# Scores of all eight attention heads from split, stacked float32r operands in a hybrid encoder block

## The chip, the core and the metric

The kernel runs on one core of a Trainium2 chip. The metric is the device time of one execution in microseconds (us). Several executions are made and the median is given; one more is recorded by the profiler, and all rows below come from that one.

## What is computed

One layer of a streaming encoder on x of 512 tokens by 1024 channels, in float32:

```python
x = x + 0.5 * swiglu_ffn(rms_norm(x, ffn1_norm), ffn1_w13, ffn1_w2)
h = rms_norm(x, mix_norm)
a, g, q, k, v, fl = split(h @ w_in)
y_conv = conv_module(a, g, ...)        # GLU, causal depthwise conv of width 31, LayerNorm, swish
y_attn = forgetting_attention(q, k, v, fl + forget_b)
y = concat(rms_norm(y_conv), rms_norm(y_attn))
x = x + y @ w_out
x = x + 0.5 * swiglu_ffn(rms_norm(x, ffn2_norm), ffn2_w13, ffn2_w2)
out = rms_norm(x, final_norm)
```

The attention has 8 heads of 64 channels. For each block of 128 queries, the scores against all keys up to the end of the block are q k^T / 8 plus the difference of a running sum of log sigmoid gates; a causal mask, a softmax and the product with the values follow. The feed-forward width is 2816.

## The kernel before, in words

Activations lie with channels on the 128 partitions and the 512 tokens in the free dimension. Every large product is made of float32r matmuls: each operand is split into a high part `h`, the value rounded to float32r, and a remainder `l`, and the product is `hi*h + hi*l + lo*h`, three matmuls for each 128 channels. Weights arrive by DMA in tiles `raw`; ScalarE writes `whi`, VectorE subtracts to get `wlo`.

The order of the work is made by a planner (`Plan`). Each operation is recorded with an estimated price; `schedule` walks through time, and gives each engine the operation that can start soonest, and among equals the one with the longest path behind it, raised by an urgency. The result is a fixed order of instructions for each engine, so an instruction whose input is late holds up everything behind it on its engine. Tiles have tags with a number of buffers, handed out in the order in which the program names them.

The stage in the middle goes, in `ORDER`, "c0 c1 c2 c3 v a0 a1 n a2 a3 w0 w1 w2 w3": four tiles of the convolution, the values and gates, attention for pairs of heads 0 and 1, the norm of the convolution, attention for pairs 2 and 3, and the output projection. Convolutions 0 and 2 are made of taps that ScalarE scales (`tap`) and GpSimd adds (`acc`); convolutions 1 and 3 (`DVE_CONV`) are taps that VectorE adds up in PSUM (`conv`), copied by ScalarE into `acc` at the end. The gates go through some twenty small steps on VectorE (`e`, `lf`, `lfs`), are transposed on TensorE (`pc`), summed (`cum`), written to memory and read back spread over the partitions (`ck`). `conv_norm` begins with the sums `ssq_mean` on TensorE over the four finished convolutions, and ends with the split tiles `yh`, `yl` in slots 0 to 7, which the first half of the output projection (`wo`) reads.

`attention(i)` handles a pair of heads, head 0 of the pair on partitions 0 to 63 and head 1 on 64 to 127. Products `pq` and `pk` make q and k for both. For pairs that are not in `STACK` each head gets a float32 q tile of 128 partitions whose other half is zero, so that one float32 matmul with the k tile `kn` of both heads gives the scores of one head. For pairs in `STACK`, the 128 partitions of a head's q tile hold the high part of q on the head's own half and the remainder on the other; k becomes two tiles, `h` with the high part of k on both halves and `l` with the remainder of k on the own half and zeros on the other. Two float32r matmuls, with `h` and with `l`, give qh kh + ql kh + qh kl. They run over at least 256 columns. The mask is added by a third, bfloat16, matmul into the same bank. A softmax follows: one VectorE operation that adds `ck` and takes the minimum (`sm<-s,ck`), an exponential on ScalarE, a scaling, transposes (`pt`) on TensorE, copies (`pT`), and the product with the values (`po`).

"r" slots: the tiles of `slot(n)` have one buffer each. Slots 0 to 21 hold the hidden activations of each half of a feed-forward; in the middle stage 0 to 15 hold `yh` and `yl`, 16 to 19 the convolutions and later k of pair 3, 14, 20 and 21 parts of the gates. Pair 2 keeps its k in the tags u0 to u3, which held the inputs of the convolution.

All operations are recorded through one helper, line 217, so the rows below are told apart by the names of their tiles, not by lines.

Of the kernel before, what the change touches and what calls it, by code (L numbers as in the profile page):

```python
# [25 lines left out]
F32R = mybir.dt.float32r  # L26
# [5 lines left out]
P = 128  # L32
T = 512
# [19 lines left out]
PIECE = 2  # L53
WARM = 10
DVE_CONV = (1, 3)
STACK = (2, 3)
STORES = {1: 0, 4: 2, 7: 5}


# [17 lines left out]
def f32(ap):  # L77
    return ap.bitcast(F32)
# [262 lines left out]
def block_kernel(ctx: ExitStack, tc, x_d, w13a, w2a, wag, wvf, wqk, wo, w13b, w2b, par_d, out_d):  # L341
# [9 lines left out]
    def tile_(shape, tag, name, bufs=1, dt=F32):  # L351
        return plan.tile(sb, shape, dt, tag, name, bufs)

    def bank(tag, name, bufs=1):
        return plan.tile(pp, [P, T], F32, tag, name, bufs)

    def product_bank(name):
        return bank("mm", name, 3)

    def slot(n, name, dt=F32):  # L360

        return tile_([P, T], f"r{n}", name, 1, dt)
# [37 lines left out]
    for w13, w2 in ((w13a, w2a), (w13b, w2b)):  # L400
# [3 lines left out]
        if w13 is w13a:  # L404
            for piece in ORDER.split():
                n = int(piece[1:] or 0)
# [6 lines left out]
    def unit():  # L413
        i = taken[0]
        taken[0] += 1
        src, idx, k, c = units[i]
        raw = tile_([P, k, c], "raw", f"raw{i}", LOADS)
        hi = tile_([P, k, c], "whi", f"whi{i}", SPLITS, F32R)
        lo = tile_([P, k, c], "wlo", f"wlo{i}", SPLITS, F32R)
        load_and_split(i, raw, hi, lo, 0, k)  # L420
        return hi, lo
# [10 lines left out]
    def split(hi, lo, src, gain):  # L432
        S.activation(hi, src, AF.Copy, scale=gain)
        V.scalar_tensor_tensor(lo, src, gain, f32(hi), ALU.mult, ALU.subtract)
# [77 lines left out]
    def product(ps, w, ah, al):  # L512

        hi, lo = w
        n = len(ah)
        first = None
        for k in range(n):
            step = plan.join("PE", first)
            if first is None:
                first = step  # L520
                if taken[0] > 3 or ready == []:
                    in_turn(step)
            PE.matmul(ps, hi[:, k], ah[k], start=k == 0, stop=False)
            PE.matmul(ps, hi[:, k], al[k], start=False, stop=False)
            PE.matmul(ps, lo[:, k], ah[k], start=False, stop=k == n - 1)
            plan.join(None)
        stream[:] = [step]
# [223 lines left out]
    def attention(i):  # L751
        rstd = mix["rstd"]
        plan.urgency = URGENT_Q
        ps = product_bank(f"pq{i}")
        product(ps, unit(), xh, xl)

        halves = [(slice(b * HD, (b + 1) * HD), slice((1 - b) * HD, (2 - b) * HD)) for b in range(2)]
        stacked = i in STACK  # L760
        qs, ks = [], []
        if stacked:
            qn = tile_([P, T], "ew", f"qn{i}", BUFS["ew"])
            V.scalar_tensor_tensor(qn, ps, -(HD ** -0.5), rstd, ALU.mult, ALU.mult)
        for b, (own, other) in enumerate(halves):
            w = tile_([P, T], f"q{i % 2}{b}", f"q{i}{b}", 1, F32R if stacked else F32)
            qs.append(w)
            if stacked:
                S.copy(w[own], qn[own])
                V.tensor_sub(w[other], qn[own], f32(w[own]))  # L770
            else:
                G.memset(w[other], 0.0)
                V.scalar_tensor_tensor(w[own], ps[own], -(HD ** -0.5), rstd[own], ALU.mult, ALU.mult)
        ps = product_bank(f"pk{i}")
        product(ps, unit(), xh, xl)
        kn = tile_([P, T], "k", f"k{i}", 2)
        V.tensor_mul(kn, ps, rstd)
        for b, (own, other) in enumerate(halves):
            if stacked:
                h, l = (tile_([P, T], f"u{2 * b + n}", f"k{i}{b}{n}", 1, F32R) if i % 2 == 0 else  # L780
                        slot(16 + 2 * b + n, f"k{i}{b}{n}", F32R) for n in range(2))
                G.memset(f32(l)[other], 0.0)
                S.copy(h[own], kn[own])
                V.tensor_sub(l[own], kn[own], f32(h[own]))
                G.tensor_copy(h[other], h[own])
                ks.append((h, l))
            else:
                ks.append((kn,))

        plan.urgency = URGENT  # L790
        ck = []
        for b in range(2):
            h = 2 * i + b
            ck.append(tile_([P, T], "ck", f"ck{h}", 2))
            with plan.urgent(500.0):
                Q.dma_start(out=ck[b], in_=cum[h // 4][h % 4:h % 4 + 1, :].spread(P))
        po = bank("misc", f"po{i}", MISC) if i == 0 else bank("cv", f"po{i}")
        for q in range(NT):
            L = (q + 1) * P
            tq = slice(q * P, L)  # L800
            pT = []
            for b in range(2):
                h = 2 * i + b
                ps = bank("s", f"s{h}_{q}", 2)
                plan.join("PE")
                n = max(L, 2 * P) if stacked else L
                for k in ks[b]:
                    PE.matmul(ps[:, :n], qs[b][:, tq], k[:, :n], start=k is ks[b][0], stop=False)
                PE.matmul(ps[:, tq], ident16, mask16, start=False, stop=True)
                plan.join(None)  # L810
                s = tile_([P, T], "sm", f"sm{h}_{q}", BUFS["sm"])[:, :L]
                st3 = tile_([P, 3], "st3", f"st{h}_{q}", 6)
                mn, sm, rs = (st3[:, n:n + 1] for n in range(3))
                V.tensor_tensor_reduce(s, ps[:, :L], ck[b][:, :L], 1.0, 3.0e38, ALU.add, ALU.min, mn)
                S.activation(s, s, AF.Exp, bias=mn, scale=-1.0, accum_out=sm)
                V.reciprocal(rs, sm)
                V.tensor_scalar(s, s, rs, None, ALU.mult)
                pt = bank("pt", f"pt{h}_{q}", PT)
                plan.join("PE")
                for kb in range(q + 1):  # L820
                    PE.transpose(pt[:, kb * P:(kb + 1) * P], s[:, kb * P:(kb + 1) * P], ident)
                plan.join(None)
                pT.append(tile_([P, T], "pT", f"pT{h}_{q}", BUFS["pT"])[:, :L])
                S.copy(pT[b], pt[:, :L])

            plan.join("PE")
            for kb in range(q + 1):
                for b in range(2):
                    h = 2 * i + b
                    PE.matmul(po[b * HD:(b + 1) * HD, tq], vt[:, kb, h * HD:(h + 1) * HD],  # L830
                              pT[b][:, kb * P:(kb + 1) * P], start=kb == 0, stop=kb == q)
            plan.join(None)
        yh[4 + i] = slot(2 * (4 + i), f"yh{4 + i}", F32R)
        yl[4 + i] = slot(2 * (4 + i) + 1, f"yl{4 + i}", F32R)
        split(yh[4 + i], yl[4 + i], po, par[:, G_OA + i:G_OA + i + 1])
        if i < 3:
            attn_stats.add(po)
        else:
            attn_stats.sum(attn_stats.square(po), False)
        plan.urgency = 0.0  # L840
# [39 lines left out]
    for piece in ORDER.split():  # L880
        n = int(piece[1:] or 0)
        if piece[0] == "c":
            conv_tile(n)
        elif piece[0] == "v":
            values()
        elif piece[0] == "a":
            attention(n)
        elif piece[0] == "n":
            plan.urgency = URGENT_LN
            rconv = conv_norm()  # L890
            plan.urgency = 0.0
        else:
            part = n // 2
            if n == 2:
                rattn = attn_stats.rstd()
            for j in range(2):
                w = unit()
                for d in (4 * (n % 2) + 2 * j, 4 * (n % 2) + 2 * j + 1):
                    w_out(part, d, w, rattn if part else rconv)
# [57 lines left out]
```

## Time and profile before

| what | value |
|---|---|
| three runs, us | 983.25, 977.52, 980.85 |
| median, us | 980.85 |
| the profiled execution, us | 982.02 |
| its span, first to last instruction, us | 979.0 |
| mean granted TensorE clock | 0.985 |
| TensorE matmul busy | 953.4 us, 97% of the span |
| VectorE busy | 518.5 us, 53% |
| ScalarE busy | 368.3 us, 38% |
| GpSimd busy | 109.8 us, 11% |
| DMA moved | 91.07 MB, mean 93 GB/s |

The share of an engine over the whole span is a mean over stages: the two feed-forwards (about 0 to 370 and 603 to 979 us) are matmul streams; the middle stage in between is where VectorE, ScalarE and GpSimd are busiest. Matmuls are pipelined and their ends are modelled, so the time between the starts of two matmuls says more than the length shown. PE is TensorE, PEld its weight loads, DVE VectorE, ACT ScalarE, POOL GpSimd. An idle time in brackets stands ahead of an instruction with what ended it. Most scores appear twice, as two records in one row ("x2"): a float32 matmul leaves two, and so do the two float32r matmuls of a stacked score.

### The profile page before, as it was taken

Reading aid. Unit: us, or ns where it says so; the run is one execution under the profiler, and the core shown is the slowest. Engines: PE = TensorE matmul, PEld = TensorE weight load, DVE = VectorE, ACT = ScalarE, POOL = GpSimd, SP = SyncE. Lnnn points to the kernel's source line nnn. Section 1 sums busy time; section 2 is a strip of 40 time slices with the busy share of each in tenths; the row PEclk is TensorE's granted clock in tenths of the full one; section 3 lists DMA queues with packets and bytes.
Section 4 is the critical chain, followed back from the end, with each engine's and each line's share of the span. In section 5 each row is a group of like instructions: output and inputs, shape, how many; then the busy total and the mean of one; then the engine's idle time right before and its main releaser. Section 6 shows DMA issues by size and latency. Waiting matters only on the chain.

```text
span 979.0 us, 11641 instructions
## 1 busy us (share of the span) xinstructions
PE 953.4 (97%) x4687; PEld 777.2 (79%) x4687; DVE 518.5 (53%) x730; ACT 368.3 (38%) x528; POOL 109.8 (11%) x102
## 2 busy tenths in 40 slices
PE   8999999999999999996999999999999999999996
PEld 7888888888888888894666777888888888888885
DVE  6544442244444444989887867444443244444433
ACT  6423221123233325666558655332321122323230
POOL 2000000000000002899432100000000000000000
PEclk9999999999999999999898999999999999999998
DMA  7222332222233222221221212222332222223202
GB/s 242 85 90 104 105 116 88 79 93 101 88 114 118 89 86 74 88 93 71 71 71 34 87 51 80 95 99 89 113 118 90 85 86 89 105 93 132 90 30 87
DMA packets 26838, 91.07 MB, mean 93 GB/s; under 512 B 2840, under 2 KB 6040, under 8 KB 26784
## 3 DMA queue, kind: packets, MB, share of 16 engines
q1 hardware_dynamic: 26784, 90.33, 27.1%
q8 instruction: 36, 0.59, 0.2%
q14 instruction: 18, 0.15, 0.0%
HBM read 88.21 MB, written 2.11 MB: 92 GB/s over the span
## 4 chain that ended last, share of the span: by engine, by line
PE 86%; DVE 6%; ACT 2%; POOL 2%; DMA 1%; issue 1%; SPq 0%; DVEq 0%; POOLq 0%; ACTq 0%
PE f2o L217 12%; PE f2g L217 12%; PE f2u L217 12%; PE f1o L217 12%; PE f1u L217 12%; PE f1g L217 12%; PE wo L217 5%; DVE conv L217 2%; POOL acc L217 2%; PE pg L217 1%; PE pa L217 1%; PE po L217 1%; DVE e L217 1%; DMA x<-x_d 1%; PE s L217 1%
## 5 line engine op out<-in xcount | busy, mean ns | idle before, releaser
L217 ACT CAST whi<-raw 128x1024 fp32r<-128x1024 f32 (+3 forms) x153 | 165.9, 1085 | 476.8 <-issue 223.7
L217 DVE TENSOR_TENSOR wlo<-raw,whi 128x1024 fp32r<-128x1024 f32 (+3 forms) x153 | 198.2, 1296 | 30.8 <-ACT whi L217 29.1
L217 POOL TENSOR_TENSOR acc<-acc,tap 128x512 f32<-128x512 f32 x60 | 88.9, 1482 | 35.0 <-ACT tap L217 30.1
L217 PE MATMUL f2o<-f2ah,whi 128*128 128x512 f32 (+1 forms) x198 | 72.7, 367 | 0.0
L217 PE MATMUL f2o<-f2al,whi 128*128 128x512 f32 (+1 forms) x198 | 72.3, 365 | 0.0
L217 PE MATMUL f2o<-f2ah,wlo 128*128 128x512 f32 (+1 forms) x198 | 72.3, 365 | 0.0
L217 PE MATMUL f1u<-xh,whi 128*128 128x512 f32 x176 | 68.8, 391 | 0.6 <-ACT xh L217 0.6
L217 PE MATMUL f1u<-xl,whi 128*128 128x512 f32 x176 | 68.7, 390 | 0.3 <-DVE xl L217 0.3
L217 PE MATMUL f2g<-xh,whi 128*128 128x512 f32 x176 | 68.7, 390 | 0.0
L217 PE MATMUL f2u<-xh,whi 128*128 128x512 f32 x176 | 68.6, 390 | 0.0
L217 PE MATMUL f1u<-xh,wlo 128*128 128x512 f32 x176 | 68.5, 389 | 0.0
L217 PE MATMUL f2g<-xh,wlo 128*128 128x512 f32 x176 | 68.5, 389 | 0.0
L217 PE MATMUL f2u<-xh,wlo 128*128 128x512 f32 x176 | 68.5, 389 | 0.0
L217 PE MATMUL f2g<-xl,whi 128*128 128x512 f32 x176 | 68.5, 389 | 0.0
L217 PE MATMUL f1o<-f1ah,whi 128*128 128x512 f32 x176 | 68.5, 389 | 0.0
L217 PE MATMUL f1o<-f1al,whi 128*128 128x512 f32 x176 | 68.5, 389 | 0.0
L217 PE MATMUL f1o<-f1ah,wlo 128*128 128x512 f32 x176 | 68.5, 389 | 0.0
L217 PE MATMUL f2u<-xl,whi 128*128 128x512 f32 x176 | 68.5, 389 | 0.0
L217 PE MATMUL f1g<-xh,whi 128*128 128x512 f32 x168 | 65.5, 390 | 0.3 <-ACT whi L217 0.3
L217 PE MATMUL f1g<-xl,whi 128*128 128x512 f32 x168 | 65.5, 390 | 0.0
L217 PE MATMUL f1g<-xh,wlo 128*128 128x512 f32 x168 | 65.5, 390 | 0.0
L217 DVE TENSOR_TENSOR f2un<-f2u,rstd_f2in 128x512 f32<-128x512 f32 x22 | 15.2, 692 | 71.8 <-PE f2u L217 71.8
(231 smaller groups left out, 1768.1 us busy)
## 6 DMA issues: line engine op xcount, KB each, us to landing
raw<-w13b SPq DMA_DIRECT2D x44, 512.0 KB, 3.2
raw<-w13a SPq DMA_DIRECT2D x42, 512.0 KB, 3.3
raw<-w2a SPq DMA_DIRECT2D x16, 704.0 KB, 4.1
raw<-w2b SPq DMA_DIRECT2D x16, 704.0 KB, 4.0
raw<-wag SPq DMA_DIRECT2D x8, 512.0 KB, 3.2
raw<-wqk SPq DMA_DIRECT2D x8, 512.0 KB, 3.2
raw<-wo SPq DMA_DIRECT2D x8, 512.0 KB, 3.2
raw<-wvf SPq DMA_DIRECT2D x4, 520.0 KB, 3.1
```

The source lines that it names most:

```text
L217: ins = getattr(target, method)(*real, **kw)
```

## The change

Pairs 0 and 1 are added to `STACK`, so that their scores are made as those of pairs 2 and 3: q and k are split, the parts are laid one above the other, and two float32r matmuls replace the float32 matmul. The tiles `h` and `l` of k for these two pairs are put into slots 0 to 3 (pair 0) and 4 to 7 (pair 1). Pair 2 keeps its k in u0 to u3 and pair 3 in slots 16 to 19.

```diff
-STACK = (2, 3)
+STACK = (0, 1, 2, 3)
...
             if stacked:
-                h, l = (tile_([P, T], f"u{2 * b + n}", f"k{i}{b}{n}", 1, F32R) if i % 2 == 0 else
+
+                h, l = (slot(4 * i + 2 * b + n, f"k{i}{b}{n}", F32R) if i < 2 else
+                        tile_([P, T], f"u{2 * b + n}", f"k{i}{b}{n}", 1, F32R) if i == 2 else
                         slot(16 + 2 * b + n, f"k{i}{b}{n}", F32R) for n in range(2))
                 G.memset(f32(l)[other], 0.0)
                 S.copy(h[own], kn[own])
```

## Rows read from the trace of the kernel before

**Rows 1.** Busy time per 20 us window; columns name engine, busy us, instructions, clock, DMA.
```profile
440.00:460.00 20.00, 16.56 (x73) 12.49 (x71) 19.89 (x32) 14.75 (x21) 18.00 (x14) 1.00 0.20 71
460.00:480.00 20.00, 14.04 (x55) 11.32 (x56) 17.26 (x29) 5.31 (x12) 8.88 (x7) 0.74 0.33 107
480.00:500.00 20.00, 17.90 (x93) 11.65 (x93) 19.16 (x49) 13.78 (x34) 12.06 (x9) 0.91 0.16 53
500.00:520.00 20.00, 20.00 (x182) 13.84 (x182) 14.55 (x33) 12.55 (x29) 6.22 (x7) 1.00 0.16 53
520.00:540.00 20.00, 17.98 (x107) 11.62 (x107) 16.10 (x39) 18.77 (x34) 5.64 (x6) 0.83 0.09 31
```

**Rows 2.** Chain that ended last, in order of time: start us, us, what.
```profile
495.21 1.13 PE s L217 x3
...
519.57 1.05 PE po L217 x16
```

**Rows 3.** Timeline of TensorE, scores and their masks: start us, us, instruction.
```profile
488.93 0.39 PE L217 MATMUL s<-k,q 128*128 128x128 f32 x2
489.15 0.22 PE L217 MATMUL s<-mask,ident 128*128 128x128 bf16 x1
...
495.21 1.02 PE L217 MATMUL s<-k,q 128*128 128x256 f32 x2 [1.99 <-DVE st L217]
496.03 0.31 PE L217 MATMUL s<-mask,ident 128*128 128x128 bf16 x1
...
506.87 1.02 PE L217 MATMUL s<-k,q 128*128 128x512 f32 x2
507.73 0.22 PE L217 MATMUL s<-mask,ident 128*128 128x128 bf16 x1
...
523.74 0.40 PE L217 MATMUL s<-k,q 128*128 128x256 f32 x2
523.98 0.23 PE L217 MATMUL s<-mask,ident 128*128 128x128 bf16 x1
...
561.48 0.61 PE L217 MATMUL s<-k,q 128*128 128x512 f32 x2
561.94 0.23 PE L217 MATMUL s<-mask,ident 128*128 128x128 bf16 x1
```

**Rows 4.** Groups by form, 380 to 660 us: operation, count, busy us, mean ns.
```profile
L217 DVE SCALAR_TENSOR_TENSOR conv<-u,par,conv 128x512 f32<-128x512 f32 x60 | 44.8, 747 | 0.7
...
L217 DVE TENSOR_TENSOR k<-k,k 64x512 fp32r<-64x512 f32 x4 | 3.4, 860 | 0.1
L217 POOL CAST k<-k 64x512 fp32r<-64x512 f32 x4 | 3.4, 857 | 12.9 <-ACT k L217 12.8
...
L217 DVE TENSOR_TENSOR q<-qn,q 64x512 fp32r<-64x512 f32 x4 | 2.7, 687 | 0.1
L217 DVE SCALAR_TENSOR_TENSOR q<-pq,rstd_f1n 64x512 f32<-64x512 f32 x4 | 2.7, 684 | 0.1
...
L217 ACT CAST k<-k 64x512 fp32r<-64x512 f32 x4 | 2.5, 620 | 0.0
...
L217 POOL MEMSET k<- 64x512 f32 x4 | 2.1, 520 | 7.4 <-DVE conv L217 7.2
...
L217 DVE SCALAR_TENSOR_TENSOR qn<-pq,rstd_f1n 128x512 f32<-128x512 f32 x2 | 1.4, 683 | 2.6 <-PE pq L217 2.6
```

**Rows 5.** Instructions on tile u: count, shortest, median and longest in ns.
```profile
L217 DVE TENSOR_TENSOR u<-an,gn x4: 693/1394/1792, 382.4 to 419.6; 128x512 f32<-128x512 f32 x4
```

**Rows 6.** Timelines of VectorE, ScalarE and TensorE: end of convolution 3, start of the mean.
```profile
501.05 0.75 DVE L217 SCALAR_TENSOR_TENSOR conv<-u,par,conv 128x512 f32<-128x512 f32 x1
...
503.14 0.58 ACT L217 COPY acc<-conv 128x512 f32<-128x512 f32 x1
...
507.88 1.08 PE L217 MATMUL ssq_mean<-acc,mean 128*32 128x128 f32 x32
```

**Rows 7.** Timeline of TensorE: the transposes of the gates.
```profile
466.46 1.12 PE L217 MATMUL pc<-ident,lfs 128*128 128x128 f32 x4 [5.46 <-DVE lfs L217]
```

## The prediction

> **What bounds the kernel now.** The page's busy times first, in the table above: TensorE is busy for 97% of the span, and most of that is the two feed-forwards, which this change does not touch. The middle stage holds the edit. There I read the table of busy time in 20 us windows [rows 1]. From 440 to 500 the engine that never rests is VectorE (19.89, 17.26 and 19.16 of 20 us), while TensorE has holes (16.56, 14.04, 17.90) and part of its time at a lower granted clock (mean 0.74 in 460 to 480, 0.91 in 480 to 500). From 500 to 520 it turns round: TensorE is busy all 20 us and VectorE 14.55. From 520 to 540 TensorE has holes again. So a saving on TensorE before about 495 is a saving on an engine that waits; one after it can be real. The chain of waits says the same: from 495.21, a score of pair 1, to the value product of pair 1 that starts at 519.57, every piece of the chain is TensorE's [rows 2].
>
> **What TensorE saves.** I take a score's cost as the time from its start to the start of the mask matmul behind it, since ends are modelled [rows 3]. At 512 columns and full clock the float32 score takes 507.73 - 506.87 = 0.86 us, and the stacked one 561.94 - 561.48 = 0.46: minus 0.40. At 128 columns float32 takes 489.15 - 488.93 = 0.22; the stacked form never runs under 256 columns and takes 523.98 - 523.74 = 0.24: plus 0.02. At 256 the float32 row is 496.03 - 495.21 = 0.82; it stands behind an idle time of 1.99 us in a window of mean clock 0.91 [rows 1], and I read it as one at the lower of the two levels, 1.2 GHz, so about 0.41 at full clock against 0.24: minus 0.17. For 384 I take the middle of the neighbours, minus 0.285. One head: 0.02 - 0.17 - 0.285 - 0.40 = -0.835 us. Pair 0, two heads: -1.67. Pair 1: its two 256-column scores ran at the lower clock (0.82 against twice 0.24, so -0.34 each), and the others as above: 0.04 - 0.68 - 0.57 - 0.80 = -2.01. Together -3.7 us, 0.4% of the run. Of that, pair 0's share falls where TensorE waits for others; pair 1's scores of 256 columns and more stand behind 495.21, on the chain: -2.05. Weight loads stay at two per score in the trace of either form.
>
> **What is added.** By form [rows 4]: VectorE gets one 128x512 qn (0.683) and loses two 64x512 q (0.684 each); it gets two q remainders (0.687) and two k remainders (0.860). A pair: 0.683 + 1.374 + 1.720 - 1.368 = 2.41 us, two pairs 4.8. ScalarE gets four casts of 0.62 a pair, 2.5 us, 5.0 in all. GpSimd gets two memsets (0.520) and two casts (0.857) a pair, 2.75 us, 5.5 in all; the q memsets that go stood in the first microseconds, off every path. GpSimd rests 11.1 us of 460 to 480 and ScalarE 14.7 [rows 1]; both hide their share there, and would pay it in full if the taps of the GpSimd convolution left no rest. The k parts now occupy slots 0 to 7, which the convolution's yh and yl write next. Those cannot be written before the convolution's norm, which only begins with its mean at 507.88 [rows 6] and has two more sums to go, when pair 1's last scores run; I cost the slots at nothing. The qn tile takes one of three "ew" buffers behind the two lfs tiles; one buffer then serves pair 0 and pair 1 in turn, and the casts hide that as long as TensorE waits for lfs anyway.
>
> **How dear the remainders are.** They are two-input subtractions that read SBUF twice, and pairs 0 and 1 are prepared while GpSimd adds convolution taps (18.00 of 20 us busy in 440 to 460). The trace has such an operation in that company: u from an and gn, same length in the free dimension, took 693 ns at best and 1792 at worst [rows 5]. So a remainder costs between 0.69 and 1.79; eight of them put the added VectorE work between 2 x (0.683 + 4 x 0.69 - 1.368) = 4.15 and 2 x (0.683 + 4 x 1.79 - 1.368) = 12.95 us. The nearest row is the k remainder, the same operation on the same shape, at 0.860, but it ran in 500 to 560, where GpSimd was busy 6.22 of 20 us and less. I therefore take 1.0, so 2 x (0.683 + 4.0 - 1.368) = 6.6 us.
> The Trainium skill has a rule that speaks against the change here ("SBUF — State Buffer", Who interferes with whom): a VectorE instruction with two SBUF inputs and a GpSimd instruction that reads SBUF exclude each other for a whole instruction. By that rule each remainder could wait out one tap, and the sum would go to its upper end; by the row of the k remainder it would be 4.8.
>
> **Where that lands.** Work that VectorE must do before 500 displaces the lowest-ranked work, the taps of convolution 3. The little steps of the forget gate alternate with whatever filler is ready, so a remainder in place of a tap (0.747 before) delays them hardly at all. The last tap starts at 501.05, its copy ends at 503.14 + 0.58 = 503.72, and the mean that needs it starts at 507.88 on TensorE [rows 6]: 4.2 us of slack, of which TensorE, 2.05 earlier, uses up half. VectorE rests 2.74 us in 460 to 480 and 0.84 in 480 to 500 [rows 1]; much of this is waiting in order, so I let about 2.1 of 6.6 vanish there. The copy then ends 4.5 later, at 508.2, and the mean starts at 508.2 in place of 507.88: +0.3 us. So TensorE's gain on the chain, -2.05, is given back as 2.35, and what pair 0 saved becomes idle time. The norm of the convolution is what the output projection waits for around 530 (TensorE's hole in 520 to 540), so its date is the stage's.
> The profiled run took 982.02 us around its span of 979.0; plus 0.3 gives 982.3. The median of the runs shown is 980.85, 1.2 lower, so I forecast **981.0 us**, no change that can be measured: a measurement of this kernel tells about 0.5%, 4.9 us, from nothing. Bounds of this case: all of -3.7 kept, 977.2; remainders at 1.79, copy 12.95 - 3.58 = 9.4 later, at 513.1, mean 5.2 later, 986.1.
>
> **Rivals.**
> (a) *All of TensorE's saving is kept.* The chain on TensorE from 495 speaks for it, and the slack of 4.2 us in front of the mean. Against it, VectorE is full until 500. It gives 980.85 - 3.7 = 977.2, and is decided by convolution 3 ending less than 2.2 us later than now.
> (b) *Faster: the hole ahead of 466 is filled.* TensorE waits 5.46 us there for lfs [rows 7], because the transposes of the gate were put into the middle of pk1, and then goes on at the lower clock. If pair 0's scores, now ready later, and the transposes are put behind more of pk1 by the planner's new times, that wait goes: -5.5 beside -3.7, so 971.7. Against it: the planner's price of a gate step does not change, and it is this price which puts the transposes too early.
> (c) *Slower: the remainders meet the taps.* If each subtraction waits for a tap, or the tap for it, convolution 3 comes out more than 4.2 + 4.9 = 9.1 us later, and the norm, the hole before the output projection and the lower clock behind it all move with it. Pure upper bound: +5.2; with one more fall of the clock (the hole in 520 to 540 goes with a mean of 0.83, at most 3.4 us lost in 20) some 2 more, so 988. It decides from a remainder of about 1.75 us. The trace has both ends of it: u at 1792 and at 693.
> (d) *The stacked form is no faster for these pairs.* Excluded by rows 3: pairs 2 and 3 run it in the same program.
>
> **How the numbers follow.** Forecast with its give-back, 0.37; (a) 0.24; (b) 0.16; (c) 0.23. Forecast and (a) both lie within 0.5%, nearly all of them: same 0.60. Faster than 975.9 is (b) with the tail of (a): 0.17. Slower than 985.8 is (c): 0.23. Each cost is below 1% of the run, but any new operation reorders every queue of the planner, which is why (b) and (c) are not smaller. The likeliest's own range is 977 to 986; the range that leaves out no more than 2 in 10 reaches into both neighbours, 975 to 988.
>
> **What would show it.** Right: scores of pairs 0 and 1 as two fp32r matmuls at 0.24 to 0.46 us; eight subtractions more on VectorE at about 1 us; the last tap of convolution 3 at 504 to 507; the mean at about 508; more idle time on TensorE between 440 and 535, by about what its busy time loses. Wrong: the mean at 505 or sooner (a), no wait of pc for lfs (b), or subtractions of 1.7 us and the mean past 512 (c). What makes me wrong outright is a new wait in order that no row of before shows, such as a score standing in TensorE's queue ahead of a GpSimd copy that stands behind taps.

## Result, and the profile after

The changed kernel takes 983.22 us (median of 20 runs, 981.47 to 986.06), the kernel before 980.19 on the same chip; the ratio is 1.0037 with a 95% interval of 1.0026 to 1.0049. That is 3.0 us more than before where I forecast no change at 981.0: inside the range and inside the bound of 0.5%, but resolved from nothing, and on the slow side. The profiled execution of the changed kernel took 985.60 us around a span of 983.9; that of before 982.02 around 979.0, so each stands about 2 us above its median, and the traces can be laid side by side. The runs of the kernel before fall into two groups by their mean granted clock (of the 78 taken beside the experiments, 35 at 0.989 or more have a median of 977.43 us and the other 43 of 981.39), so its median lies between the two.

All of the difference arises in the middle stage. Up to 440 us the two traces lie within 0.2 us of each other (`pq` starts at 437.87 before and 438.04 after). The first matmul of the second feed-forward (`f2g`) starts at 602.93 before and 608.30 after; from there to the end of the span it is 376.1 and 375.6 us.

The busy times on the page of the kernel after:
```profile
PE 955.3 (97%) x4687; PEld 780.5 (79%) x4687; DVE 522.3 (53%) x736; ACT 372.9 (38%) x536; POOL 114.4 (12%) x106
```
VectorE rose by 3.8 us, ScalarE by 4.6, GpSimd by 4.6; TensorE did not fall. The windows of 20 us, columns as in [rows 1]:
```profile
440.00:460.00 20.00, 15.77 (x67) 12.05 (x65) 19.84 (x33) 12.98 (x19) 16.00 (x11) 0.98 0.21 73
460.00:480.00 20.00, 18.09 (x74) 14.23 (x74) 19.06 (x38) 12.43 (x22) 13.68 (x11) 0.77 0.33 107
480.00:500.00 20.00, 17.89 (x108) 12.82 (x107) 19.50 (x35) 15.09 (x33) 13.92 (x11) 0.91 0.23 79
500.00:520.00 20.00, 17.88 (x139) 12.82 (x138) 17.71 (x42) 11.72 (x25) 6.63 (x7) 0.93 0.16 53
520.00:540.00 20.00, 17.58 (x131) 11.58 (x130) 15.24 (x24) 17.15 (x28) 7.55 (x8) 0.90 0.08 27
...
560.00:580.00 20.00, 18.08 (x119) 12.89 (x119) 12.64 (x40) 9.99 (x27) 0.00 (x0) 0.91 0.17 54
580.00:600.00 20.00, 18.74 (x117) 13.98 (x112) 11.85 (x17) 10.28 (x15) 0.00 (x0) 0.91 0.15 52
```
Against [rows 1], TensorE is busier from 460 to 480 (18.09, was 14.04), and has idle time and a lower clock where it had none: 500 to 520 (17.88 at 0.93, was 20.00 at 1.00), and 560 to 600, where before was busy all 40 us at 1.00. A mean between 0.5 and 1.00 is time at 1.2 GHz mixed with time at 2.4.

The scores do what the change says. Timeline of TensorE, which answers to [rows 3]:
```profile
506.08 0.39 PE L217 MATMUL s<-k,q 128*128 128x256 f32 x2
506.32 0.23 PE L217 MATMUL s<-mask,ident 128*128 128x128 bf16 x1
...
510.91 0.61 PE L217 MATMUL s<-k,q 128*128 128x384 f32 x2
511.37 0.23 PE L217 MATMUL s<-mask,ident 128*128 128x128 bf16 x1
...
514.12 0.73 PE L217 MATMUL s<-k,q 128*128 128x512 f32 x2 [0.33 <-DVE st L217]
514.69 0.23 PE L217 MATMUL s<-mask,ident 128*128 128x128 bf16 x1
```
From score to mask it is 0.24 us at 256 columns, 0.46 at 384 and 0.57 at 512 here, in a window of mean clock 0.93; pair 1's last score, at 518.69, took 1.00. Summed by this measure, the sixteen scores of pairs 0 and 1 take 9.97 us before and 6.89 after: 3.1 us less. The added operations, groups by form from 380 to 660 us, which answer to [rows 4]:
```profile
L217 DVE TENSOR_TENSOR q<-qn,q 64x512 fp32r<-64x512 f32 x8 | 6.8, 855 | 0.2
...
L217 DVE TENSOR_TENSOR k<-k,k 64x512 fp32r<-64x512 f32 x8 | 5.8, 730 | 2.1 <-ACT k L217 1.9
```
The subtractions are not dear: 0.73 us a k remainder and 0.86 a q remainder, near the low ends.

What is new is where they stand. Timelines of VectorE, ScalarE and TensorE, around the end of convolution 3, which answer to [rows 6]:
```profile
498.08 1.16 DVE L217 TENSOR_TENSOR q<-qn,q 64x512 fp32r<-64x512 f32 x1
...
499.16 0.74 DVE L217 SCALAR_TENSOR_TENSOR conv<-u,par,conv 128x512 f32<-128x512 f32 x1
...
500.65 0.59 ACT L217 COPY acc<-conv 128x512 f32<-128x512 f32 x1
500.79 0.84 DVE L217 TENSOR_TENSOR q<-qn,q 64x512 fp32r<-64x512 f32 x1
...
502.31 1.08 PE L217 MATMUL ssq_mean<-acc,mean 128*32 128x128 f32 x32
502.35 0.67 DVE L217 TENSOR_TENSOR k<-k,k 64x512 fp32r<-64x512 f32 x1
...
504.25 0.69 DVE L217 TENSOR_TENSOR k<-k,k 64x512 fp32r<-64x512 f32 x1
504.93 0.49 PE L217 MATMUL s<-k,q 128*128 128x256 f32 x2
```
The four remainders of pair 1 stand behind the taps, the first of them ahead of the last tap only. Their high parts had been there since 466.5 (q) and 475.3 (k). So the last tap comes at 499.16 (501.05 before), the mean at 502.31 (507.88 before, 5.6 us earlier), and pair 1's first score at 504.93 (488.93 before, 16 us later). ScalarE shows what follows from it (its timeline; `sm` of 128x128 and 128x512 are the first and last exponentials of a pair, `yh<-po` its output):
```profile
508.01 0.40 ACT L217 ACTIVATE sm<-sm,st 128x128 f32<-128x128 f32 x1 [4.29 <-DVE st L217]
...
515.48 0.37 ACT L217 ACTIVATE rc_ln<-ssq_ln,eps 128x128 f32<-128x128 f32 x1
...
521.92 1.28 ACT L217 ACT_TABLE_LOAD   x1
523.21 1.52 ACT L217 ACTIVATE acc<-acc,par 128x512 f32<-128x512 f32 x2
...
530.27 0.72 ACT L217 ACTIVATE sm<-sm,st 128x512 f32<-128x512 f32 x1
...
538.96 0.69 ACT L217 ACTIVATE yh<-po,par 128x512 fp32r<-128x512 f32 x1 [0.45 <-PE po L217]
...
542.38 0.40 ACT L217 ACTIVATE sm<-sm,st 128x128 f32<-128x128 f32 x1
```
Before, pair 1 had its exponentials from 495.19 and its output at 520.64, ahead of the norm's root (`rc_ln`, 522.64). Now the norm's root and its activation (`acc<-acc`) cut into pair 1's softmax, each with a table load of 1.28 us to it and another back, and pair 1 comes out at 538.96. No table load was added: ScalarE's timeline has six between 510 and 545 us in either trace. Before, they cut into pair 2's softmax, and only pair 3 was left whole behind the norm; now they cut into pair 1's, and pairs 2 and 3 are both left. Pair 2 starts at 542.38 (524.82 before), and the last output of attention comes at 580.60 (574.49 before). TensorE then runs dry; three of the five rows with a wait in its timeline from 570 to 584:
```profile
574.01 0.55 PE L217 MATMUL pt<-ident,sm 128*128 128x128 f32 x3 [0.46 <-ACT pT L217]
575.18 1.12 PE L217 MATMUL pt<-ident,sm 128*128 128x128 f32 x4 [0.62 <-ACT pT L217]
...
581.82 0.60 PE L217 MATMUL ssq_attn<-sq_attn,ones 128*32 128x128 f32 x8 [1.26 <-ACT sq_attn L217]
```
None of the five stands in the trace before, where TensorE is busy for all of 540 to 620. The chain that ended last, which in [rows 2] was TensorE's alone from 495.21 to 519.57, goes through other engines now:
```profile
523.21 1.52 ACT acc L217 x2
...
571.98 0.69 DVE sm L217
...
580.60 0.69 ACT yh L217
```
And the hole of [rows 7] is smaller, while the product ahead of it waits longer for a weight remainder, 3.91 us where it was 1.78 at 460.51:
```profile
460.55 0.80 PE L217 MATMUL pk<-xh,wlo 128*128 128x512 f32 x1 [3.91 <-DVE wlo L217]
...
463.99 1.12 PE L217 MATMUL pc<-ident,lfs 128*128 128x128 f32 x4 [1.36 <-DVE lfs L217]
```

### The profile page after: what moved, and what is told of

The parts are those of the page before. It is cut to its first block, busy times and chain, and to the rows that moved or that the text cites. A ratio compares the mean times of both kernels' runs of the same rounds, so it can differ in the third digit from the quotient of the medians.

```text
span 983.9 us, 11669 instructions
## 1 busy us (share of the span) xinstructions
PE 955.3 (97%) x4687; PEld 780.5 (79%) x4687; DVE 522.3 (53%) x736; ACT 372.9 (38%) x536; POOL 114.4 (12%) x106
## 4 chain that ended last, share of the span: by engine, by line
PE 88%; DVE 6%; POOL 2%; ACT 2%; issue 1%; DMA 1%; SPq 0%; DVEq 0%; ACTq 0%; POOLq 0%
PE f2o L217 12%; PE f2g L217 12%; PE f2u L217 12%; PE f1o L217 12%; PE f1u L217 12%; PE f1g L217 12%; PE wo L217 5%; DVE conv L217 2%; POOL acc L217 2%; PE pk L217 1%; PE pq L217 1%; DVE wlo L217 1%; PE s L217 1%; PE pg L217 1%; PE pa L217 1%
```

## The experiments

Two questions: is the extra time that of the added work, or of the order in which the planner put it; and if of the order, which operation's place is it? Ratios are to the kernel before on the same chip, with 95% intervals.

**One pair at a time.** First pair 0 alone, then pair 1 alone, beside pairs 2 and 3.
```
-STACK = (0, 1, 2, 3)
+STACK = (0, 2, 3)      # and (1, 2, 3) in the second
```


> Only pair 0 gets the stacked scores beside pairs 2 and 3 (STACK = 0, 2, 3); pair 1 keeps float32 scores. Theory A (order): the loss of the change comes from pair 1 alone, whose remainders stand behind the taps of convolution 3 on VectorE, so that its first scores wait from about 489 to 505. Without that, pair 1 starts before 495, the output norm of the attention (rb_attn) comes at or before 581, and the time is that of before or up to 3 us less: 977 to 981. Theory B (work): each pair costs its added VectorE work, so pair 0 alone gives half the loss, about 981.7. Theory C (any new operation reshuffles the queues): no relation to the change of both, anywhere in 976 to 987.

> Only pair 1 gets the stacked scores beside pairs 2 and 3 (STACK = 1, 2, 3). Theory A (order): the remainders of pair 1 again stand behind convolution 3, its first scores come after 500, and the loss is all there: 983 to 985. Theory B (work): half the loss, about 981.7. Theory C: no relation, 976 to 987.


Pair 0 alone: 977.12 us, 0.9972 (0.9958 to 0.9986). Pair 1 alone: 977.54, 0.9981 (0.9966 to 0.9996). Each half of the change is a little faster than before, and both together are slower. The costs of the added operations would add up; these do not. The first was expected at 977 to 981 if the order of pair 1's work is to blame. The second was foreseen by neither theory: 983 to 985 by the order, 981.7 by the added work. So a late start of pair 1 is not enough by itself. In the first, pair 1's first exponential is at 496.13 and its output at 516.31; in the second they are at 501.23 and 532.58, still clear of pair 2. Only with both is pair 1 later than 537.

**Is the saving on TensorE worth anything?** From the changed kernel, the scores of pairs 0 and 1 issued twice, with q halved; and from the kernel before, the same scores as two float32r matmuls without the casts and remainders.
```
-for j, k in enumerate(ks[b]):
+for j, k in enumerate(ks[b] * (2 if i < 2 else 1)):    # q scaled by 1/2 for i < 2
```
```
-w = tile_([P, T], f"q{i % 2}{b}", f"q{i}{b}", 1, F32R if stacked else F32)
+w = tile_([P, T], f"q{i % 2}{b}", f"q{i}{b}", 1, F32R)  # k too; ks[b] * 2 where not stacked
```


> The changed kernel, but the two float32r matmuls of a score are issued twice for pairs 0 and 1, into the same accumulation, with q scaled by half of the factor, so that the scores are the same and TensorE spends about what it spent on float32. What is left of the change is the preparation. Theory A: TensorE's saving was worth nothing, since TensorE waits for pair 1's attention, so 983 to 985. Theory B, with the saving of 3.7 us real and the preparation dearer than it: 986 to 988. Theory C: 978 to 988 without order.

> The kernel before, with the scores of pairs 0 and 1 made by two float32r matmuls over at least 256 columns from q and k rounded to float32r, both with the same operands and q scaled by half, so without the remainder products and without any preparation: TensorE's saving alone. If the saving lands on the chain it gives 976 to 978 (minus 2 to 4 us); if TensorE only waits longer for VectorE it gives 979 to 981. Theory C: 976 to 986.


Scores issued twice: 983.79 us, 1.0039 (1.0023 to 1.0056), the same as the changed kernel. The scores added are worth 0.24 us at 128 and 256 columns, 0.46 at 512 [rows 3] and some 0.35 between them, for four heads 5.2 us; none of it can be seen at the end. Cheap scores without their preparation: 978.21, 0.9989 (0.9972 to 1.0006), a gain of 1 us that can't be told from none and is at most 2.7, of a saving forecast at 3.7. So the price of the scores explains neither the gain that is missing nor the loss.

**The order alone.** The changed kernel, in which the planner gives the remainders an urgency of 200, so that they go ahead of the taps: for all eight; for pair 1's four; for pair 0's four.
```
+before_u, plan.urgency = plan.urgency, 200.0 if i < 2 else plan.urgency   # i == 1; i == 0
 V.tensor_sub(w[other], qn[own], f32(w[own]))
+plan.urgency = before_u     # and the same around the subtraction for l
```


> The changed kernel with all its work, but the eight remainder subtractions of pairs 0 and 1 get an urgency of 200, so that VectorE takes them before the taps of convolution 3. Theory A2 (order, after the runs with one pair): the loss comes from pair 1's attention, which starts after the taps (first exponential at 508 instead of 495) and is then cut by the convolution's norm on ScalarE, so that two pairs instead of one stay behind the norm, about 19 us each. With the remainders first, the first exponential of pair 1 comes before 500, pair 2 starts before the norm's square root, the last yh of the attention comes at or before 574, and the time is 976 to 979. Theory B (work): the added work of VectorE, ScalarE and GpSimd is all still there, so 983 as after the change, or more since convolution 3 ends later.

> The same, but only the four subtractions of pair 1 get the urgency. Theory A2: these are the ones that matter; 976 to 980. Theory B: 983 or more. If it is pair 0's remainders that matter, it stays at 983.

> The changed kernel in which only the four subtractions that make pair 0's remainders carry the urgency of 200; those of pair 1 stay behind the taps of convolution 3 as in the changed kernel. Theory C (the changed kernel loses its time through pair 1 alone, whose remainders come too late, and what went wrong with all eight urgent was pair 0's part of it): pair 1's scores stay late, its first exponential after 503 instead of 495 to 496 with pair 1's urgent; the first score of pair 0 waits over 2 us in TensorE's queue near 460, as it did with all eight (3.60 us at 459.80); so nothing is won back, ratio to the kernel before 1.003 to 1.008. Rival D (what went wrong with all eight urgent was the number of subtractions ahead of the taps, four or eight, whichever pair they serve): half of them gives what pair 1's four gave, the mean of the convolution's norm at 505 to 509 and a ratio of 0.996 to 1.000.


Pair 1's four: 978.40 us, 0.9980 (0.9966 to 0.9994). Nothing is taken out of the changed kernel; four subtractions go to another place, and the others move in consequence. The median is 4.8 us below that of the changed kernel (5.6 by the two ratios), level with the versions that prepare one pair only. Its ScalarE timeline has pair 1 ahead of the norm again, and pair 2 started ahead of the norm's activation, as before the change:
```profile
495.56 0.39 ACT L217 ACTIVATE sm<-sm,st 128x128 f32<-128x128 f32 x1
...
517.04 0.69 ACT L217 ACTIVATE yh<-po,par 128x512 fp32r<-128x512 f32 x1 [0.67 <-PE po L217]
...
520.81 0.37 ACT L217 ACTIVATE rc_ln<-ssq_ln,eps 128x128 f32<-128x128 f32 x1
...
524.42 0.40 ACT L217 ACTIVATE sm<-sm,st 128x128 f32<-128x128 f32 x1
...
528.46 1.52 ACT L217 ACTIVATE acc<-acc,par 128x512 f32<-128x512 f32 x2
```
TensorE is busy again for all of 540 to 620 (two of the windows of 20 us):
```profile
560.00:580.00 20.00, 20.00 (x137) 14.95 (x136) 13.68 (x31) 10.73 (x21) 0.00 (x0) 1.00 0.25 80
580.00:600.00 20.00, 20.00 (x126) 14.27 (x125) 16.08 (x23) 10.78 (x16) 0.00 (x0) 1.00 0.21 64
```
All eight: 987.38 us, 1.0067 (1.0047 to 1.0087), the slowest of the study, though pair 1's first exponential came early, at 494.56, as it should. The time missed its expectation, 976 to 979. Two other dates had moved, seen in TensorE's timeline:
```profile
459.80 1.23 PE L217 MATMUL s<-k,q 128*128 128x256 f32 x2 [3.60 <-POOL k L217]
...
517.05 0.65 PE L217 MATMUL ssq_mean<-acc,mean 128*32 128x128 f32 x8 [2.06 <-ACT acc L217]
...
541.51 0.80 PE L217 MATMUL wo<-yl,whi 128*128 128x512 f32 x1 [1.14 <-DVE yl L217]
```
Pair 0's first score was put early into TensorE's queue and stood there 3.60 us for GpSimd's copy of k. And with eight subtractions and pair 1's exponentials ahead of its last taps, convolution 3 was copied at 516.41 (503.14 before), so its part of the mean came at 517.05 and the output projection only at 539.87 (532.92 before).

Pair 0's four: 983.55 us, 1.0037 (1.0020 to 1.0054), as the changed kernel. Pair 1's first exponential is at 508.14 again, and the score waits 3.61 us for GpSimd's copy at 459.43, as with all eight. So moving four subtractions helps only where they are pair 1's. (Its profiled execution, 980.22 us, was the fastest of its 11 runs; the dates in the table below are of that one.)

**The norm's own urgency.** If the norm, early as it is, harms pair 1, taking its urgency away should help the changed kernel, and only that.
```
-URGENT_LN = 200.0
+URGENT_LN = 20.0
```


> The changed kernel with the urgency of the convolution's norm at 20 instead of 200, below that of the attention (50); the remainders stay where the change left them. Theory A2 with the cut as its second half: pair 1's last exponentials now stand before the norm's square root and silu, so pair 1 ends earlier than 539 and the last yh before 580: 978 to 982. If the late start of pair 1 alone decides, it stays at 983. If the norm's date decides (as the prediction had it), it is slower: 985 to 988.

> The kernel before with the urgency of the convolution's norm at 20: the control for the run with the changed kernel. In the kernel before pair 1 is done and pair 2 begun before the norm, so theory A2 expects little: 978 to 982. A gain as large as that of the changed kernel would mean that the norm's urgency has nothing to do with the change.


In the changed kernel: 981.76 us, 1.0020 (1.0004 to 1.0036), 1.5 us under the changed kernel's median, with an interval that overlaps its own, so this gain can't be told from none. In the kernel before: 984.52, 1.0035 (1.0021 to 1.0049), where 978 to 982 was expected: there the same edit costs 3.6 us, and its output projection starts 7.0 us later (539.94). So the pair of runs bears the theory out in sign at most. Letting the norm yield gives pair 1 its softmax back (all its exponentials stand ahead of `rc_ln` at 519.57, its output at 526.06), and the last output of attention is at 568.96, 11.6 us earlier than in the changed kernel; but then pairs 2 and 3 run with too little other work beside them. TensorE's rows with a wait:
```profile
549.71 1.09 PE L217 MATMUL po<-pT,vt 128*64 128x128 f32 x14 [0.77 <-ACT pT L217]
553.19 0.61 PE L217 MATMUL s<-k,q 128*128 128x384 f32 x2 [0.63 <-DVE st L217]
554.37 0.61 PE L217 MATMUL s<-k,q 128*128 128x384 f32 x2 [0.49 <-DVE st L217]
555.96 0.73 PE L217 MATMUL s<-k,q 128*128 128x512 f32 x2 [0.79 <-DVE st L217]
```

**All versions by their dates** (us, profiled executions; the ratio is of the timed runs):

| version | ratio | pair 1: first exponential, output | first `wo` | last output of attention | first `f2g` |
|---|---|---|---|---|---|
| before | 1 | 495.19, 520.64 | 532.92 | 574.49 | 602.93 |
| changed | 1.0037 | 508.01, 538.96 | 525.62 | 580.60 | 608.30 |
| pair 0 only | 0.9972 | 496.13, 516.31 | 530.77 | 568.29 | 598.82 |
| pair 1 only | 0.9981 | 501.23, 532.58 | 524.96 | 574.00 | 600.17 |
| changed, scores twice | 1.0039 | 507.22, 542.11 | 523.40 | 578.72 | 604.87 |
| before, cheap scores | 0.9989 | 494.86, 522.27 | 527.38 | 574.15 | 601.22 |
| changed, all eight first | 1.0067 | 494.56, 525.69 | 539.87 | 579.60 | 610.13 |
| changed, pair 1's first | 0.9980 | 495.56, 517.04 | 531.56 | 574.32 | 601.39 |
| changed, pair 0's first | 1.0037 | 508.14, 537.27 | 524.88 | 576.76 | 602.91 |
| changed, norm not urgent | 1.0020 | 505.37, 526.06 | 528.14 | 568.96 | 604.25 |
| before, norm not urgent | 1.0035 | 495.22, 518.42 | 539.94 | 569.15 | 607.15 |

Two dates, with bounds set after the fact, sort all but one of them. Where pair 1's output is at 537 or later, or the output projection starts at 539.8 or later, the ratio is 1.0035 or more; where neither holds it is 1 or less. The exception is the changed kernel with the norm not urgent, late on neither date and yet at 1.0020; the waits from 549 to 557 are the only thing in its trace that I can name for it.

## Why the prediction was right and wrong

**What TensorE saves: nearly right in size, worth less than thought.** The sixteen scores took 3.1 us less where I forecast 3.7; pair 1's two scores of 512 columns, for one, took 0.57 and 1.00 us and not 0.46. The saving is not seen in the total. I had let pair 0's share go and kept 2.05 us of pair 1's on the chain; issuing all the scores twice cost nothing measurable, so in the changed kernel that share isn't on the path either.

**What is added: right, and cheaper than the value taken.** For pairs 0 and 1, the groups of 440 to 506 us have four q remainders with 3.4 us and four k remainders with 2.7. With two `qn` at 0.68 more and four 64x512 q at 0.684 less, VectorE's added work is 3.4 + 2.7 + 1.36 - 2.74 = 4.7 us (3.8 by the page), where I took 6.6 and bounded it by 4.15 and 12.95. The longest took 1.16 us, so rival (c), remainders of 1.75 us, did not come about in the changed kernel. By the rule of the Trainium skill that I weighed ("SBUF — State Buffer", Who interferes with whom) a remainder could have waited out a GpSimd tap. The trace agrees for two of the eight: those at 498.08 and 500.79 took 1.16 and 0.84 us and ended 0.56 and 0.54 us after GpSimd's additions had ended, at 498.68 and 501.09. The two at 453.45 and 456.74 took 0.69 us each though GpSimd was busy with taps there (16.00 of 20 us). So the price hangs on where a subtraction falls beside GpSimd's work: in the version with the norm not urgent, the one at 454.19 took 1.84 us.

**The step that failed** is the first sentence of "Where that lands": "Work that VectorE must do before 500 displaces the lowest-ranked work, the taps of convolution 3." The taps are not the lowest-ranked work beside the remainders. The planner ranks by the length of the path behind an operation, and behind a tap lies the norm with all of the output projection, while behind a remainder of pair 1 lies only that pair's attention and the second half of the projection. By the printed code's own ranking the last tap of convolution 3 has 400.8, and pair 1's remainders, their small urgency included, have 377.6, below even `k` and `qn` of pair 2 (379.1 and 378.4). So it was the remainders that gave way. Everything I drew from it has the wrong sign: the last tap, forecast for 504 to 507, came at 499.16, and the mean, forecast for about 508, at 502.31. That is the sign named for rival (a), a mean at 505 or sooner; its time of 977.2 did not come with it.

**"Its date is the stage's"** failed with it. The norm came 5.6 us earlier, the output projection 7.3, and the stage ended 5.4 us later. There are two dates: the norm's, and that of attention, whose last output releases the second half of the output projection. I priced only the first, and put a later start of pair 1 at nothing. That the time still fell inside the range, 2.2 us above the forecast, is luck: the delay that I summed did not occur, and another that was not in the sum took its place. When all eight remainders were put ahead of the taps, what I had described did happen (convolution 3 copied 13 us late, a ratio of 1.0067): the mechanism exists, but not in the order that the planner made.

**Rival (b)** was half right: the transposes wait 1.36 us in place of 5.46, with the product ahead of them 5.27 in place of 7.24. The gates themselves ended earlier (`lf` at 462.62, was 464.88), for a reason told in the last section. The 2 us won there are lost behind 500. **The warning at the end**, a new wait in order that no row of before shows, was the right kind: it is pair 1's scores behind subtractions behind taps, in VectorE's queue and not GpSimd's. The score behind a GpSimd copy came only in the versions with pair 0's remainders first.

**What is shown and what is argued.** Shown: the place of pair 1's four subtractions, with what moves in its wake, makes the difference of 4.8 us; the added work and the scores' price do not. Argued from the dates: that it goes by the norm's work on ScalarE cutting into pair 1's softmax, and by the two pairs left behind the norm. Two pairs alone are not enough: the version with pair 1 only also starts pair 2 late, at 536.75, and is not slower. A rival stays open in part: that any new order lands anywhere from 976 to 987 us (theory C of the first expectations). Against it speak the scores issued twice and pair 0's remainders first: both move other work, leave pair 1 late, and keep the ratio (1.0039 and 1.0037, the changed kernel 1.0037). For it speak the versions that came out other than expected. How the 4.8 us divide between idle time of TensorE and its clock (median of the timed runs' mean clock 0.985 in the changed kernel, 0.988 with pair 1's remainders first) stays open.

The best of the versions are pair 0 only and the full change with pair 1's subtractions first. Both beat both kernels, by 0.2 to 0.3% against before; neither is faster than the fastest runs of before.

## What to carry to other kernels

Where a planner orders the work, price a new operation by its rank first and its duration second: ask what stands ahead of it while it is ready, and who waits for it. Follow every branch that joins at the end of a stage, not only the one that was last before; here one branch gained 5.6 us and the other lost 6. And when a change of several like parts disappoints, try the parts one at a time and the same parts in another order: both were cheap here, and each gave back what the change had cost.

## What the runs showed of the hardware

Where GpSimd's additions ran beside VectorE instructions that read two SBUF tiles, both took longer. GpSimd's share: instructions on tile `acc` in the changed kernel (count: shortest, median and longest in ns, first and last start), first from 449 to 459 us, where the two q subtractions of 0.69 us lie, then from 475 to 500:
```profile
L217 POOL TENSOR_TENSOR acc<-acc,tap x5: 1292/1811/2214, 449.8 to 456.7; 128x512 f32<-128x512 f32 x5
...
L217 POOL TENSOR_TENSOR acc<-acc,tap x12: 1268/1294/1963, 476.6 to 499.8; 128x512 f32<-128x512 f32 x12
```
GpSimd's copies of k ranged from 0.61 to 1.49 us for one and the same 64x512 shape.

VectorE's share shows best in the little steps of the gates, which are one operation on one shape (timelines of GpSimd and VectorE in the changed kernel):
```profile
449.78 8.77 POOL L217 TENSOR_TENSOR acc<-acc,tap 128x512 f32<-128x512 f32 x5 [0.86 <-ACT tap L217]
...
457.46 1.14 DVE L217 SCALAR_TENSOR_TENSOR e<-e,e 128x32 f32<-128x32 f32 x1
...
459.18 0.18 DVE L217 SCALAR_TENSOR_TENSOR e<-e,e 128x32 f32<-128x32 f32 x1
...
462.75 1.15 POOL L217 CAST k<-k 64x512 fp32r<-64x512 f32 x1 [4.20 <-ACT k L217]
```
While GpSimd added, until 458.55, five of these steps took 0.79 to 1.27 us each. The three from 459.18 to 461.18, while GpSimd was idle, took 0.18. In the kernel before, GpSimd added without a stop until 465.61, and all eight took 0.61 to 1.27. So it was GpSimd standing still for its copy of k, which waited for ScalarE, that let the gates end 2.3 us earlier.
